# Smaller trips through HBM for the turned hidden rows, queued splits of q and k, and bias tiles loaded on another queue

## The chip, the cores and the metric

The kernel runs on one core of a Trainium2 chip. The metric is the device time of one execution in microseconds, as the median of several. The core has a matrix engine (TensorE, PE in the rows), three engines for the rest (VectorE or DVE, ScalarE or ACT, GpSimd or POOL), an engine that only issues transfers here (SyncE or SP), and 16 DMA engines that all queues share. Each engine works off its own list of instructions in order. A DMA is issued by one of the engines: SP loads the weights, ACT and POOL issue the others.

## The reference

Two networks stand behind each other, of two layers each, on 256 positions of width 1024, all in float32. A layer is a feed-forward part with factor 0.5, a mixer, and a second feed-forward part, each added to the stream x:

```python
def swiglu(x, w_in, w_out):
    gu = x @ w_in                        # 1024 -> 2 x 2816
    g, u = jnp.split(gu, 2, axis=-1)
    return (jax.nn.silu(g) * u) @ w_out  # 2816 -> 1024

x = x + 0.5 * swiglu(rms_norm(x, ffn1_norm[l]), ffn1_w_in[l], ffn1_w_out[l])
x = x + mixer(rms_norm(x, mix_norm[l]), mix_w_in[l], ...)
x = x + 0.5 * swiglu(rms_norm(x, ffn2_norm[l]), ffn2_w_in[l], ffn2_w_out[l])
```

There are thus eight feed-forward parts. The mixer of the first network projects x to q, k, v (512 columns each), to the input of a Fourier part and to two gates, and its attention over 8 heads adds a learned table before the softmax:

```python
s = jnp.einsum('brjqhd,brjuvhd->brjhquv', qg, k_win) * scale + bias[None]  # bias gathered from rpb
s = jnp.where(col_ok, s, -jnp.inf)
p = jax.nn.softmax(s, axis=-1)
```

The mixer of the second network (three kinds of attention) is not touched by the change.

## The kernel before

A product of float32 matrices is made of three matmuls on operands split in a high and a low half (`mm3`, L143). For the weights, `unit` (L111) loads 4 rows of 128 of k by 512 columns into a tile `raw` on SP's queue, and for each pair of k, called a weight tile here, ACT casts the high half `whi` (L341) and DVE subtracts it for the low half `wlo` (L342). `whi` and `wlo` have four buffers each in the parts that matter, so ACT's next cast waits until TensorE is through with an older tile. A weight tile feeds 12 matmuls of 512 columns. SP's loads go ahead as far as the pool of `raw`, four tiles, allows.

**Ticks.** Work that needs no TensorE is queued with `later(fn, ticks)` (L66). Each weight tile is one tick: `advance` (L69) runs at most one entry that is due. `drain` (L62) runs all that is left. What is run at a tick is only recorded there: a scheduler fixes the final order of each engine's list when the program is built.

**The turn.** The second product of a feed-forward part needs h = silu(g)·u with its 2816 columns on the partitions. `turned` (L86) does this without TensorE: DVE transposes blocks of 32×32 into `hB` (L94, one per half t of the positions, one buffer), POOL writes `hB` to HBM (`hop`, L96), and POOL reads it back in the other arrangement (`hT`, L97). That is a trip. `queue_t` (L76) queues the splits `hhi` (ACT, L341) and `hlo` (DVE, L342) of what came back, 7 ticks later. `queue_x` (L201) does the same for half of x between the parts.

**The feed-forward part** (`ffn`, L244). Six chunks of columns of h, five of 512 and one of 256; a chunk of 512 takes 8 weight tiles, four for g and four for u. `GROUPS` (L18) says at which chunk a new tile of h begins: chunks 0 and 1 are turned together, 2 and 3 together (2048 columns of `hB`, 1 MB each way), 4 and 5 alone. `sl` (L272) is silu(g) on ACT, and `h` (L274) its product with u on DVE. The second product has 22 rows of k of h for each half of the output columns; it is written as 16, a drain, and 6.

**The neighbourhood mixer** (`mixer1`). For each pair of heads p, `bias1` (L428) loads a part of the learned table with four DMAs on ACT's queue into a tile `rawb` of the weights' own `raw` pool, and adds the mask on DVE at once (L439). Pairs 0 and 1 are made before the projections, 2 and 3 inside the attention loop. q and k make trips as h does, into `qT` and `kT`; their splits (`qh`, `kzh` on ACT, `kq` on DVE) stand after the drain that ends the projections, though the scheduler may bring them forward.

Of the kernel before, what the change touches and what calls it, by code (L numbers as in the profile page):

```python
# [10 lines left out]
F32 = mybir.dt.float32  # L11
# [3 lines left out]
ALU = mybir.AluOpType  # L15
AX = mybir.AxisListType.X

GROUPS = (0, 2, 4, 5)  # L18
P = 128
T = 2  # L20
D = 1024
# [5 lines left out]
class Net:  # L27
# [46 lines left out]
                return fn()  # L74

    def queue_t(self, h, nk, hhi, hlo, k0):  # L76
        hv = self.turned(lambda t: h[t], nk, self.b("hT", n=2048))
        lag = 7 if nk > 2 else 6
        step = min(nk, 4)
        for i in range(0, nk, step):  # L80
            for t in range(T):
                o = lambda d: d[:, k0 + i : k0 + i + step, t * P : (t + 1) * P].rearrange(
                    "p k (q j) -> p k q j", j=32)
                self.later(lambda hi=o(hhi), lo=o(hlo), s=hv[:, i : i + step, t]: self.split(hi, lo, s), lag)

    def turned(self, src, nk, tile):  # L86
        nc = self.nc
        n = nk * 256
        hop = self.hop.tile([4, P, nk * 64], F32, name=self.nm("hop"), tag=f"hop{nk}")
        hb = self.b("hB", n=2048, bufs=1)[:, :n]  # L90
        ov = hb.rearrange("p (c k t j) -> p k c t j", c=4, t=T, j=32)

        def turn(t):
            nc.vector.transpose(ov[:, :, :, t, :], src(t)[:, : nk * P].rearrange("p (k i c) -> p k c i", c=4, i=32))  # L94
            if t == T - 1:
                nc.gpsimd.dma_start(out=hop.rearrange("q (i c) n -> (q i) (c n)", c=4), in_=hb)  # L96
                nc.gpsimd.dma_start(out=tile[:, :n].rearrange("p (q n) -> p q n", q=4),  # L97
                                    in_=hop.rearrange("q p n -> p q n"))

        for t in range(T):  # L100
            self.later(lambda t=t: turn(t))
        return tile[:, :n].rearrange("p (q k t j) -> p k t q j", q=4, t=T, j=32)
# [98 lines left out]
    def queue_x(self, li):  # L201
        hv = self.turned(lambda t: self.x[:, t, :512], 4, self.xtile())

        def part(k):
            g = self.gcol[:, li, k : k + 1] if isinstance(li, int) else li[:, k : k + 1]
            for t in range(T):
                o = lambda d: d[:, k, t * P : (t + 1) * P].rearrange("p (q j) -> p q j", j=32)
                self.split(o(self.xhi), o(self.xlo), hv[:, k, t], scale=g)

        for k in range(4):  # L210
            self.later(lambda k=k: part(k), 7)

    def xt_half(self, n, li):
        nc = self.nc
# [29 lines left out]
    def ffn(self, w_in, w_out, nxt):  # L244
        nc = self.nc
        rs = None
        self.open()
        self.xtile = lambda: self.b("hT", n=2048)
        self.more(2)
        hhi = self.big.tile([P, 22, T * P], F32R, name=self.nm("hhi"), tag="hhi")  # L250
        hlo = self.big.tile([P, 22, T * P], F32R, name=self.nm("hlo"), tag="hlo")
        self.hold = True
        for c in range(6):
            if c < 5:
                pg = self.dense(self.xhi, self.xlo, KD, [(w_in, c * 512, 512)])
                pu = self.dense(self.xhi, self.xlo, KD, [(w_in, DFF + c * 512, 512)])
                w = 512
                gs, us = pg, pu
            else:
                pp = self.dense(self.xhi, self.xlo, KD, [(w_in, 2560, 256), (w_in, DFF + 2560, 256)])  # L260
                w = 256
                gs, us = pp, [q[:, 256:512] for q in pp]
            if rs is None:
                rs = self.rstd()
            if c == 0:
                self.hold = False
                self.drain()
            if c in GROUPS:
                h, c0 = [self.b("h", n=1024, bufs=4) for _ in range(T)], c
            for t in range(T):  # L270
                sl = self.b("sl", bufs=3)
                nc.scalar.activation(sl[:, :w], gs[t][:, :w], AF.Silu, scale=rs[:, t : t + 1])  # L272
                o = (c - c0) * 512
                nc.vector.scalar_tensor_tensor(h[t][:, o : o + w], us[t][:, :w], rs[:, t : t + 1], sl[:, :w],  # L274
                                               op0=ALU.mult, op1=ALU.mult)
            if c == 5 or c + 1 in GROUPS:
                self.queue_t(h, (o + w) // P, hhi, hlo, c0 * 4)
        for n in range(2):
            ps = self.dense(hhi, hlo, 16, [(w_out, n * 512, 512)], last=False)
            self.drain()  # L280
            self.dense(hhi, hlo, 6, [(w_out, n * 512, 512)], ps=ps, k0=16, first=False)
            for t in range(T):
                xs = self.x[:, t, n * 512 : (n + 1) * 512]
                nc.vector.scalar_tensor_tensor(xs, ps[t], 0.5, xs, op0=ALU.mult, op1=ALU.add)
            self.after(n, nxt)
        self.xtile = None
        self.more(0)
        self.close()
# [120 lines left out]
class Mix1:  # L409
# [18 lines left out]
    def bias1(self, l, p):  # L428
        nc = self.nc
        rp = self.a["rpbp"]  # L430
        bt = self.raw.tile([P, 4, 512], F32, name=self.nm("rawb"), tag="raw").rearrange("p a b -> p (a b)")[:, :768]
        bv = bt.rearrange("p (h e k) -> p h e k", h=2, e=6)
        for half in range(2):
            for h in range(2):
                src = bass.AP(tensor=rp.tensor, offset=((l * 8 + 2 * p + h) * 15 + 5 - half) * 127,
                              ap=[[1, 64], [127, 6], [1, 64]])
                nc.scalar.dma_start(out=bv[half * 64 : half * 64 + 64, h], in_=src)
        bias = self.big.tile([P, 768], F32, name=self.nm("bias"), tag="bias", bufs=3)
        nc.vector.tensor_tensor(bias.rearrange("p (h k) -> p h k", k=64)[:, :, ::-1],  # L439
                                bt.rearrange("p (h k) -> p h k", k=64),  # L440
                                self.cmask.unsqueeze(1).broadcast_to([P, 12, 64]), op=ALU.add)
        return bias

    def mixer1(self, l, nxt):
        nc, a, tc = self.nc, self.a, self.tc
# [12 lines left out]
        qh, vn = tl("qh", [P, 4, 256], F32R), tl("vn", [P, T, 512])  # L458
        u = big.tile([P, KD, 256], F32R, name=self.nm("u"), tag="mhi").rearrange("p (h t a) b -> p h t (a b)", h=2, t=2)
        uhi, ulo = u[:, 0], u[:, 1]  # L460
        bt = [self.bias1(l, p) for p in range(2)]
        self.zpad(kzh.bitcast(F32))
        self.zpad(kzl.bitcast(F32))
        rs = rq = None
        for c in range(4):
            ps = self.dense(self.xhi, self.xlo, KD, [(w_in, c * 512, 512)])
            if c == 0:
# [3 lines left out]
            if c < 2:  # L471
                h = []
# [6 lines left out]
                        nc.vector.tensor_scalar(out=ht, in0=ps[t], scalar1=sc, scalar2=None, op0=ALU.mult)  # L479
                    h.append(ht)  # L480
                turned = self.turned(lambda t, h=h: h[t], 4, qT if c == 0 else kT)
                qv, kv = (turned, None) if c == 0 else (qv, turned)
            elif c == 2:
                for t in range(T):
                    sc = rs[:, t : t + 1]
# [8 lines left out]
                    nc.vector.scalar_tensor_tensor(ulo[:, t], ps[t], sc, uhi[:, t].bitcast(F32),  # L494
                                                   op0=ALU.mult, op1=ALU.subtract)
        self.drain()
        for t in range(T):
            o = lambda d: d[:, :, t * P : (t + 1) * P].rearrange("p k (q j) -> p k q j", j=32)
            self.split(o(qh), o(ql), qv[:, :, t])
            for i in range(2):  # L500
                r = slice(64 * i, 64 * i + 64)
                self.split(o(kzh[:, :, i])[r], o(kzl[:, :, i])[r], kv[r, :, t])
        ohi, olo = tl("ohi", [P, 4, 256], F32R), tl("olo", [P, 4, 256], F32R)
        for p in range(4):
            if p % 2 == 0:
                ona = self.b("ona").rearrange("p (t c) -> p t c", t=T)
            for t in range(T):
                sc = self.psum(self.at)
                e0 = (2 - 2 * t) * 64
                tq = slice(t * P, (t + 1) * P)  # L510
                self.mm3(sc, 512, qh[:, p, tq], ql[:, p, tq], flat(kzh[:, p]), flat(kzl[:, p]), True, True)
                bias = [bt[p][:, h * 384 + e0 : h * 384 + e0 + 256] for h in range(2)]
                po, rc = self.attend(sc, 2, lambda j, st: vn[:, st, (2 * p + j) * 64 : (2 * p + j + 1) * 64], bias)
                nc.vector.tensor_tensor(ona[:, t, (p % 2) * P : (p % 2 + 1) * P].rearrange("p (j d) -> p j d", j=2),
                                        po, rc.unsqueeze(2).broadcast_to([P, 2, 64]), op=ALU.mult)
            if p < 2:
                bt.append(self.bias1(l, p + 2))
            if p % 2 == 1:
                self.tr4(lambda j, t: ona[:, t, j * P : (j + 1) * P],
                         ohi[:, p - 1 : p + 1, :].rearrange("p a b -> p (a b)"),  # L520
                         olo[:, p - 1 : p + 1, :].rearrange("p a b -> p (a b)"))
# [646 lines left out]
```

## Time and profile before

| | before |
| --- | --- |
| median of 3 runs, us | 2278.05 (2275.5, 2278.05, 2285.15) |
| the profiled execution, us | 2291.64 |
| its span, us | 2289.8 |
| granted TensorE clock, mean | 0.996 |
| busy: TensorE / VectorE / ScalarE / GpSimd | 99% / 68% / 50% / 3% |
| chain that ended last: TensorE, issue, DMA | 85%, 7%, 5% |
| of it the trips: hT from hop, hop from hB | 2%, 2% |

The profiled execution lies 13.6 us above the median of the runs. Busy time of TensorE is modelled, since matmuls overlap; how many were started in a stretch tells more than its share. The granted clock is a share of full speed: 1.00 is 2.4 GHz, 0.50 is 1.2 GHz.

### The profile page before, as it was taken

The numbers are of one execution on the slowest core, as the hardware profiler recorded it, in microseconds if no ns is written. First come the engines' busy times: TensorE is split into PE (matmuls) and PEld (weight loads), VectorE is DVE, ScalarE is ACT, GpSimd is POOL, SyncE is SP. The second block draws the span as 40 slices with busy tenths as digits, with TensorE's granted clock in tenths as the row PEclk, the third lists the DMA queues.
The fourth block names the chain that finished last, engine by engine and source line by source line (L and its number), as shares of the span: only waits on it lengthen the run. The fifth ranks groups of instructions, "written<-read, shape, count | busy, mean of one in ns | idle before, by whom it ended". The sixth has DMA issues, their size and how long they took to land.

```text
span 2289.8 us, 27621 instructions
## 1 busy us (share of the span) xinstructions
PE 2260.2 (99%) x10446; PEld 1861.1 (81%) x10446; DVE 1547.2 (68%) x2549; ACT 1148.8 (50%) x1674; POOL 78.3 (3%) x133
## 2 busy tenths in 40 slices
PE   9999999999999999999999999999999999999999
PEld 7877888888788888887888887787887888778787
DVE  5666766666576776666666896765656668877564
ACT  5445545445444555445544555544444455455443
POOL 0001000000000000000000000000000000000000
PEclk9999999999999999999999999999999999999999
DMA  7767555776676745676766533467666755325673
GB/s 263 250 230 231 176 167 181 250 246 204 210 258 208 233 160 180 229 259 209 238 233 214 181 117 129 137 211 241 230 202 224 254 185 174 119 89 198 214 254 130
DMA packets 241669, 464.68 MB, mean 203 GB/s; under 512 B 22176, under 2 KB 47392, under 8 KB 239488
## 3 DMA queue, kind: packets, MB, share of 16 engines
q1 hardware_dynamic: 212272, 397.44, 52.6%
q0 software_dynamic: 14320, 60.69, 7.4%
q10 hardware_dynamic: 14944, 4.79, 1.1%
q8 instruction: 82, 1.34, 0.2%
q14 instruction: 51, 0.42, 0.1%
HBM read 433.00 MB, written 29.88 MB: 202 GB/s over the span
## 4 chain that ended last, share of the span: by engine, by line
PE 85%; issue 7%; DMA 5%; ACT 2%; DVE 1%; ACTq 0%; DVEq 0%; POOLq 0%
PE ps L146 26%; PE ps L145 26%; PE ps L147 26%; DMA hT<-hop 2%; PE ps L403 2%; DMA hop<-hB 2%; PE ps L396 1%; PE ps L891 1%; ACT whi L341 1%; DVE wlo L342 1%; PE ps L683 1%; PE ps L220 1%; PE ps L836 0%; PE ps L240 0%; ACT hhi L341 0%
## 5 line engine op out<-in xcount | busy, mean ns | idle before, releaser
L342 DVE TENSOR_TENSOR wlo<-raw,whi 128x1024 fp32r<-128x1024 f32 (+2 forms) x754 | 906.4, 1210 | 540.0 <-ACT whi L341 522.2
L341 ACT CAST whi<-raw 128x1024 fp32r<-128x1024 f32 (+2 forms) x754 | 777.9, 1044 | 780.9 <-PE ps L147 730.5
L146 PE MATMUL ps<-wlo,xhi 128*128 128x512 f32 (+2 forms) x2048 | 800.3, 392 | 8.3 <-DVE wlo L342 8.2
L145 PE MATMUL ps<-whi,xhi 128*128 128x512 f32 (+2 forms) x2048 | 786.2, 393 | 8.8 <-ACT whi L341 8.4
L147 PE MATMUL ps<-whi,xlo 128*128 128x512 f32 (+2 forms) x2048 | 789.6, 390 | 0.0
L146 PEld LDWEIGHTS ps<-wlo,xhi 128*128 128x128 f32 x2048 | 386.4, 189 | 90.8 <-DVE wlo L342 12.4
L145 PEld LDWEIGHTS ps<-whi,xhi 128*128 128x128 f32 x2048 | 385.3, 189 | 90.2 <-ACT whi L341 11.3
L147 PEld LDWEIGHTS ps<-whi,xlo 128*128 128x128 f32 x2048 | 386.6, 189 | 77.8 <-issue 0.5
L146 PE MATMUL ps<-wlo,hhi 128*128 128x512 f32 x704 | 273.9, 389 | 0.0
L147 PE MATMUL ps<-whi,hlo 128*128 128x512 f32 x704 | 273.9, 389 | 0.0
L145 PE MATMUL ps<-whi,hhi 128*128 128x512 f32 x704 | 271.3, 389 | 0.0
L145 PEld LDWEIGHTS ps<-whi,hhi 128*128 128x128 f32 x704 | 132.1, 188 | 27.6
L146 PEld LDWEIGHTS ps<-wlo,hhi 128*128 128x128 f32 x704 | 132.1, 188 | 27.4
L147 PEld LDWEIGHTS ps<-whi,hlo 128*128 128x128 f32 x704 | 132.1, 188 | 27.3
L94 DVE STREAM_TRANSPOSE hB<-h 128x1024 f32<-128x1024 f32 (+2 forms) x72 | 98.8, 1385 | 5.7 <-DMA hop<-hB 5.4
L342 DVE TENSOR_TENSOR hlo<-hT,hhi 128x512 fp32r<-128x512 f32 (+1 forms) x96 | 58.4, 643 | 56.5 <-ACT hhi L341 56.2
L341 ACT CAST hhi<-hT 128x512 fp32r<-128x512 f32 (+1 forms) x96 | 49.8, 582 | 87.8 <-DMA hT<-hop 87.8
L272 ACT ACTIVATE sl<-ps,rstd 128x512 f32<-128x512 f32 (+1 forms) x96 | 62.3, 651 | 50.9 <-PE ps L147 46.8
L96 POOL DMA_DIRECT2D hop<-hB x43 | 23.6, 548 | 1756.9 <-ACT whi L341 862.3
L391 ACT ACTIVATE pr<-ms,nmx 128x256 f32<-128x256 f32 (+1 forms) x112 | 51.3, 460 | 43.5 <-DVE nmx L386 38.7
L274 DVE SCALAR_TENSOR_TENSOR h<-ps,rstd,sl 128x512 f32<-128x512 f32 (+1 forms) x96 | 65.1, 697 | 2.9 <-PE ps L147 1.8
L97 POOL DMA_DIRECT2D hT<-hop x39 | 29.6, 758 | 184.6 <-DMA hop<-hB 103.6
(352 smaller groups left out, 1707.1 us busy)
## 6 DMA issues: line engine op xcount, KB each, us to landing
raw<-in_ffn_w_gu_dram SPq DMA_DIRECT2D x80, 1024.0 KB, 5.2
raw<-in_ffn_w_in_dram SPq DMA_DIRECT2D x79, 1024.0 KB, 5.2
raw<-in_ffn_w_out_dram SPq DMA_DIRECT2D x40, 1024.0 KB, 5.3
raw<-in_ffn_w_down_dram SPq DMA_DIRECT2D x40, 1024.0 KB, 5.1
raw<-in_mix_w_in_dram SPq DMA_DIRECT2D x32, 1024.0 KB, 6.5
raw<-in_w_gate_dram SPq DMA_DIRECT2D x24, 1024.0 KB, 5.2
hop<-hB POOLq DMA_DIRECT2D x16, 1024.0 KB, 5.9
hT<-hop POOLq DMA_DIRECT2D x16, 1024.0 KB, 6.2
```

What stands on the lines that cost most here:

```text
L94: nc.vector.transpose(ov[:, :, :, t, :], src(t)[:, : nk * P].rearrange("p (k i c) -> p k c i", c=4, i=32))
L96: nc.gpsimd.dma_start(out=hop.rearrange("q (i c) n -> (q i) (c n)", c=4), in_=hb)
L97: nc.gpsimd.dma_start(out=tile[:, :n].rearrange("p (q n) -> p q n", q=4), in_=hop.rearrange("q p n -> p q n"))
L145: mm(ps[:, :n], lhsT=lh, rhs=hi, start=start, stop=False)
L146: mm(ps[:, :n], lhsT=lh, rhs=lo, start=False, stop=False)
L147: mm(ps[:, :n], lhsT=ll, rhs=hi, start=False, stop=stop)
L272: nc.scalar.activation(sl[:, :w], gs[t][:, :w], AF.Silu, scale=rs[:, t : t + 1])
L274: nc.vector.scalar_tensor_tensor(h[t][:, o : o + w], us[t][:, :w], rs[:, t : t + 1], sl[:, :w], op0=ALU.mult, op1=ALU.mult)
L341: self.nc.scalar.copy(hi, src)
L342: return self.nc.vector.tensor_sub(lo, src, hi.bitcast(F32))
L391: nc.scalar.activation(pr[:, s], src[:, s], AF.Exp, bias=nm[:, j : j + 1], accum_out=den[:, j : j + 1])
L403: nc.tensor.matmul(po[:, j * 64 : (j + 1) * 64], lhsT=pt[:, q], rhs=v(j, st), start=(st == 0), stop=(st == ns - 1))
```

## The change

Every chunk of h is turned by its own trip: `GROUPS` holds all six, a trip of chunks 0 to 3 is 512 KB each way instead of 1 MB for two chunks, and `hT`, `hB` and `h` are half as wide. The lag of the splits is 8 ticks everywhere. The second product is one run of 22 rows without the drain in it. In the mixer, `rawb` becomes a tile of its own with one buffer, its DMAs go to POOL's queue, the mask addition is a step of its own (`mask1`) that is queued at ticks 6 and 10, then stands after the drain and after the first pair of heads, and each starts the next pair's load. The splits of q are queued at 9 ticks and those of k at 7.

```diff
-GROUPS = (0, 2, 4, 5)
+GROUPS = (0, 1, 2, 3, 4, 5)
...
-        hv = self.turned(lambda t: h[t], nk, self.b("hT", n=2048))
-        lag = 7 if nk > 2 else 6
+        hv = self.turned(lambda t: h[t], nk, self.b("hT", n=1024))
+        lag = 8
...
-        hb = self.b("hB", n=2048, bufs=1)[:, :n]
+        hb = self.b("hB", n=1024, bufs=1)[:, :n]
...
-            self.later(lambda k=k: part(k), 7)
+            self.later(lambda k=k: part(k), 8)
...
-                h, c0 = [self.b("h", n=1024, bufs=4) for _ in range(T)], c
+                h, c0 = [self.b("h", bufs=4) for _ in range(T)], c
...
-            ps = self.dense(hhi, hlo, 16, [(w_out, n * 512, 512)], last=False)
-            self.drain()
-            self.dense(hhi, hlo, 6, [(w_out, n * 512, 512)], ps=ps, k0=16, first=False)
+            ps = self.dense(hhi, hlo, 22, [(w_out, n * 512, 512)])
...
-        bt = self.raw.tile([P, 4, 512], F32, name=self.nm("rawb"), tag="raw").rearrange("p a b -> p (a b)")[:, :768]
+        bt = self.b("rawb", 768, 1)
...
-                nc.scalar.dma_start(out=bv[half * 64 : half * 64 + 64, h], in_=src)
+                nc.gpsimd.dma_start(out=bv[half * 64 : half * 64 + 64, h], in_=src)
+        return bt
+
+    def mask1(self, bt):
...
-        bt = [self.bias1(l, p) for p in range(2)]
+        bt, rb = [], [self.bias1(l, 0)]
+
+        def masked():
+            bt.append(self.mask1(rb.pop()))
+            if len(bt) < 4:
+                rb.append(self.bias1(l, len(bt)))
+
+        for n in (6, 10):
+            self.later(masked, n)
...
+                    for t in range(T):
+                        self.later(lambda t=t: split_q(t), 9)
...
+                    for t in range(T):
+                        self.later(lambda t=t: split_k(t), 7)
...
         self.drain()
-        for t in range(T):
-            o = lambda d: d[:, :, t * P : (t + 1) * P].rearrange("p k (q j) -> p k q j", j=32)
-            self.split(o(qh), o(ql), qv[:, :, t])
...
+        masked()
...
-            if p < 2:
-                bt.append(self.bias1(l, p + 2))
+            if p == 0:
+                masked()
```

ScalarE's list in the first feed-forward part, where the second trip of before is split (chunks 2 and 3, `hT_798`) and where the one of chunk 3 is after (`hT_818`). Before:

```order
L341 CAST whi_883<-raw_877 128x1024
L341 CAST whi_913<-raw_911 128x1024
L272 ACTIVATE sl_951<-ps_801,rstd_306 128x512
L341 CAST whi_919<-raw_911 128x1024
L272 ACTIVATE sl_954<-ps_802,rstd_306 128x512
L341 CAST whi_965<-raw_962 128x1024
L341 CAST hhi_150<-hT_798 128x4x128 x4
L341 CAST whi_971<-raw_962 128x1024
L341 CAST whi_1004<-raw_1001 128x1024
```

After:

```order
L339 CAST whi_905<-raw_899 128x1024
L339 CAST whi_935<-raw_933 128x1024
L272 ACTIVATE sl_971<-ps_821,rstd_306 128x512
L339 CAST whi_939<-raw_933 128x1024
L272 ACTIVATE sl_974<-ps_822,rstd_306 128x512
L339 CAST hhi_150<-hT_818 128x4x128 x2
L339 CAST whi_985<-raw_982 128x1024
L339 CAST whi_991<-raw_982 128x1024
L339 CAST whi_1023<-raw_1020 128x1024
```

Four casts that stood behind the first weight tile after the two `sl` are now two, directly behind the second `sl`.

GpSimd's list in the first neighbourhood mixer, from the clearing of `kzh` and `kq` (MEMSET) to the trip of k. Before:

```order
L349 MEMSET kzh_1499 64x4x256
L350 MEMSET kzh_1499 64x4x256
L349 MEMSET kq_1500 64x4x256
L350 MEMSET kq_1500 64x4x256
L96 DMA hop_1619<-hB_1620 128x1024
L97 DMA qT_1501<-hop_1619 128x4x256
L546 DMA h_2276<-in_mix_gate_bias_dram 128x512
L546 DMA h_2352<-in_mix_gate_bias_dram 128x512
L546 DMA h_2428<-in_mix_gate_bias_dram 128x512
L96 DMA hop_1699<-hB_1700 128x1024
L546 DMA h_2504<-in_mix_gate_bias_dram 128x512
L97 DMA kT_1502<-hop_1699 128x4x256
```

After, from the last MEMSET on (four loads of `rawb_1524`, the first pair's, stand ahead of the MEMSETs):

```order
L348 MEMSET kq_1518 64x4x256
L435 DMA rawb_1645<-in_rpbp_dram 64x6x64 x4
L96 DMA hop_1628<-hB_1629 128x1024
L435 DMA rawb_1732<-in_rpbp_dram 64x6x64 x4
L566 DMA h_2294<-in_mix_gate_bias_dram 128x512
L566 DMA h_2370<-in_mix_gate_bias_dram 128x512
L97 DMA qT_1519<-hop_1628 128x4x256
L566 DMA h_2446<-in_mix_gate_bias_dram 128x512
L96 DMA hop_1715<-hB_1716 128x1024
L566 DMA h_2522<-in_mix_gate_bias_dram 128x512
L435 DMA rawb_1888<-in_rpbp_dram 64x6x64 x4
L97 DMA kT_1520<-hop_1715 128x4x256
```

Three groups of four loads now stand between the trips of q and k, and the trip back of k is the last of them all.

VectorE's list in the same mixer, from the third chunk's tiles on: `bias` is the mask addition, `kq` the low halves of q and k. Before:

```order
L479 TENSOR_SCALAR h_1697<-ps_1622,rstd_1597 128x512
L94 STREAM_TRANSPOSE hB_1700<-h_1695 128x4x4x32
L94 STREAM_TRANSPOSE hB_1700<-h_1697 128x4x4x32
L342 TENSOR_TENSOR wlo_1748<-raw_1741,whi_1747 128x1024
L342 TENSOR_TENSOR kq_1500<-qT_1501,qh_1503 128x4x128 x2
L439 TENSOR_TENSOR bias_1923<-rawb_1918,cmask 128x12x64
L342 TENSOR_TENSOR wlo_1782<-raw_1779,whi_1781 128x1024
L342 TENSOR_TENSOR wlo_1786<-raw_1779,whi_1785 128x1024
L342 TENSOR_TENSOR wlo_1816<-raw_1813,whi_1815 128x1024
L489 TENSOR_SCALAR vn_1504<-ps_1702,rstd_1597 128x512
L342 TENSOR_TENSOR wlo_1820<-raw_1813,whi_1819 128x1024
```

After:

```order
L497 TENSOR_SCALAR h_1713<-ps_1631,rstd_1606 128x512
L94 STREAM_TRANSPOSE hB_1716<-h_1711 128x4x4x32
L340 TENSOR_TENSOR wlo_1771<-raw_1761,whi_1770 128x1024
L94 STREAM_TRANSPOSE hB_1716<-h_1713 128x4x4x32
L340 TENSOR_TENSOR wlo_1805<-raw_1802,whi_1804 128x1024
L340 TENSOR_TENSOR wlo_1811<-raw_1802,whi_1810 128x1024
L441 TENSOR_TENSOR bias_1886<-rawb_1732,cmask 128x12x64
L340 TENSOR_TENSOR wlo_1843<-raw_1840,whi_1842 128x1024
L514 TENSOR_SCALAR vn_1522<-ps_1718,rstd_1606 128x512
L340 TENSOR_TENSOR wlo_1851<-raw_1840,whi_1850 128x1024
L340 TENSOR_TENSOR kq_1518<-qT_1519,qh_1521 128x4x128 x2
```

The third pair's mask addition stands two weight tiles later than before, and the split of q, which stood ahead of it, four tiles later.

## Rows read from the trace of the kernel before

**Rows 1.** Stretches of 15 us: busy time and instruction count of each engine, TensorE's granted clock.

```profile
80.00:95.00 15.00, 15.00 (x68) 12.43 (x67) 7.75 (x8) 7.19 (x8) 0.00 (x0) 1.00 0.79 271
116.00:131.00 15.00, 12.89 (x56) 10.14 (x55) 11.12 (x13) 7.13 (x9) 0.45 (x1) 1.00 0.49 165
225.00:240.00 15.00, 12.24 (x47) 9.60 (x46) 8.69 (x10) 7.12 (x11) 0.76 (x1) 0.89 0.98 282
603.00:618.00 15.00, 12.60 (x42) 9.53 (x42) 9.76 (x11) 7.64 (x10) 0.00 (x0) 0.77 0.42 140
728.00:743.00 15.00, 13.88 (x60) 10.90 (x59) 12.02 (x27) 7.21 (x12) 0.14 (x1) 1.00 0.88 328
1556.00:1571.00 15.00, 13.30 (x57) 10.44 (x56) 10.98 (x12) 9.79 (x12) 0.00 (x0) 1.00 0.58 193
1738.00:1753.00 15.00, 12.79 (x49) 9.91 (x48) 9.76 (x11) 7.96 (x10) 0.00 (x0) 0.89 0.47 146
2166.00:2181.00 15.00, 12.16 (x53) 9.48 (x52) 10.79 (x12) 8.27 (x11) 0.00 (x0) 1.00 0.48 156
```

**Rows 2.** Waits of TensorE: us in total, times, longest.

```profile
PE ps L145 <- ACT whi L341: 8.9, 9, 2.1
PE ps L146 <- DVE wlo L342: 8.2, 9, 2.8
```

**Rows 3.** Waits of ScalarE, the same columns.

```profile
ACT hhi L341 <- DMA hT<-hop: 87.8, 32, 6.0
```

**Rows 4.** ScalarE's timeline, first FFN: start, us, instruction, count, idle before and releaser.

```profile
110.26 0.68 ACT L272 ACTIVATE sl<-ps,rstd 128x512 f32<-128x512 f32 x1
114.75 1.05 ACT L341 CAST whi<-raw 128x1024 fp32r<-128x1024 f32 x1 [3.80 <-PE ps L147]
119.68 2.18 ACT L341 CAST hhi<-hT 128x512 fp32r<-128x512 f32 x4 [3.87 <-DMA hT<-hop]
121.77 1.99 ACT L341 CAST whi<-raw 128x1024 fp32r<-128x1024 f32 x2
```

**Rows 5.** TensorE's timeline, same stretch.

```profile
118.63 0.39 PE L145 MATMUL ps<-whi,xhi 128*128 128x512 f32 x1
...
122.86 0.49 PE L145 MATMUL ps<-whi,xhi 128*128 128x512 f32 x1 [1.35 <-ACT whi L341]
```

**Rows 6.** VectorE's timeline, first FFN: end of the fourth chunk, a subtraction, turn of the fifth.

```profile
97.94 1.41 DVE L274 SCALAR_TENSOR_TENSOR h<-ps,rstd,sl 128x512 f32<-128x512 f32 x2
...
125.25 1.22 DVE L342 TENSOR_TENSOR wlo<-raw,whi 128x1024 fp32r<-128x1024 f32 x1
...
128.17 2.08 DVE L94 STREAM_TRANSPOSE hB<-h 128x512 f32<-128x512 f32 x2
```

**Rows 7.** ScalarE's timeline, the fifth chunk's split.

```profile
139.71 1.15 ACT L341 CAST hhi<-hT 128x512 fp32r<-128x512 f32 x2 [4.55 <-DMA hT<-hop]
```

**Rows 8.** The same turn and split in a later FFN, on VectorE and ScalarE.

```profile
1180.95 2.08 DVE L94 STREAM_TRANSPOSE hB<-h 128x512 f32<-128x512 f32 x2
...
1194.20 1.14 ACT L341 CAST hhi<-hT 128x512 fp32r<-128x512 f32 x2 [6.05 <-DMA hT<-hop]
```

**Rows 9.** VectorE's groups by form: busy us, mean ns.

```profile
L94 DVE STREAM_TRANSPOSE hB<-h 128x512 f32<-128x512 f32 x24 | 25.0, 1077 | 0.0
```

**Rows 10.** Second neighbourhood mixer: VectorE's turn of k.

```profile
748.64 2.07 DVE L94 STREAM_TRANSPOSE hB<-h 128x512 f32<-128x512 f32 x2
```

**Rows 11.** The DMA issued at 757.11 us in that mixer.

```profile
kT<-hop POOLq DMA_DIRECT2D x1, 512.0 KB, 8.5
```

**Rows 12.** First neighbourhood mixer, VectorE's timeline: a mask addition.

```profile
227.97 0.96 DVE L439 TENSOR_TENSOR bias<-rawb,cmask 128x768 f32<-128x768 f32 x1 [4.68 <-DMA rawb<-in_rpbp_dram]
```

**Rows 13.** Tile rawb: DMA to landing.

```profile
DMA to landing us min/median/max: 2.7/4.2/11.4
```

**Rows 14.** TensorE's timeline in the first attention.

```profile
270.99 0.44 PE L396 MATMUL ps<-ident,pr 128*128 128x128 f32 x2 [0.86 <-ACT pr L391]
```

**Rows 15.** Tile hT: durations in ns (min/median/max) of its DMA issues on GpSimd.

```profile
L97 POOL DMA_DIRECT2D hT<-hop x39: 754/758/766, 67.0 to 2235.1; - x39
```

More of the change, by code (lines that the diff above doesn't have):

```diff
@@ L247, in ffn @@
         self.open()
-        self.xtile = lambda: self.b("hT", n=2048)
+        self.xtile = lambda: self.b("hT", n=1024)
         self.more(2)
@@ L436, in bias1 @@
                               ap=[[1, 64], [127, 6], [1, 64]])
-                nc.scalar.dma_start(out=bv[half * 64 : half * 64 + 64, h], in_=src)
+                nc.gpsimd.dma_start(out=bv[half * 64 : half * 64 + 64, h], in_=src)
+        return bt
+    def mask1(self, bt):
+        nc = self.nc
         bias = self.big.tile([P, 768], F32, name=self.nm("bias"), tag="bias", bufs=3)
@@ L464, in mixer1, with split_k @@
         rs = rq = None
+        part = lambda d, t: d[:, :, t * P : (t + 1) * P].rearrange("p k (q j) -> p k q j", j=32)
+        split_q = lambda t: self.split(part(qh, t), part(ql, t), qv[:, :, t])
+        def split_k(t):
+            for i in range(2):
+                r = slice(64 * i, 64 * i + 64)
+                self.split(part(kzh[:, :, i], t)[r], part(kzl[:, :, i], t)[r], kv[r, :, t])
         for c in range(4):
@@ L481, in mixer1 @@
                 turned = self.turned(lambda t, h=h: h[t], 4, qT if c == 0 else kT)
-                qv, kv = (turned, None) if c == 0 else (qv, turned)
+                if c == 0:
+                    qv = turned
+                    for t in range(T):
+                        self.later(lambda t=t: split_q(t), 9)
+                else:
+                    kv = turned
+                    for t in range(T):
+                        self.later(lambda t=t: split_k(t), 7)
             elif c == 2:
@@ L496, in mixer1 @@
         self.drain()
-        for t in range(T):
-            o = lambda d: d[:, :, t * P : (t + 1) * P].rearrange("p k (q j) -> p k q j", j=32)
-            self.split(o(qh), o(ql), qv[:, :, t])
-            for i in range(2):
-                r = slice(64 * i, 64 * i + 64)
-                self.split(o(kzh[:, :, i])[r], o(kzl[:, :, i])[r], kv[r, :, t])
+        masked()
         ohi, olo = tl("ohi", [P, 4, 256], F32R), tl("olo", [P, 4, 256], F32R)
```

## The prediction, made blind

> **What bounds the kernel now.** I read first how many matmuls TensorE starts in stretches of equal length, because its busy share of 99% is modelled and hides small gaps. An undisturbed stretch of 15 us shows 68 matmuls, and the stretches with a gap 42 to 60 [rows 1]. A matmul is shown 0.39 us long, so a stretch counts those of 15.4 us, and one is started every 15.4 / 68 = 0.2267 us; a weight tile, 12 matmuls, takes 2.72 us. TensorE is the bound nearly everywhere, and what can be won lies in the gaps. Its own waits come next: 8.9 us for `whi` and 8.2 us for `wlo`, nine times each [rows 2]. So it never waits for a trip directly, but for a cast or subtraction that stands behind something else on ScalarE or VectorE. ScalarE's waits then name what: 87.8 us for `hT`, in 32 places [rows 3]. Only a few of these 32 cost TensorE anything, and the timeline of one shows when.
>
> In the first FFN ScalarE casts a weight tile at 114.75, then stands at the four `hhi` casts until the trip lands, 3.87 us, casts them in 2.18 us, and casts the next tile only at 121.77 [rows 4]. The tile that begins at 118.63 is used up 2.72 us later, at 121.4 and TensorE starts again at 122.86, 1.35 us of waiting by its own row, with a second wait for `wlo` behind [rows 5]. The cast of 114.75 feeds a tile that begins at 118.63: it was ready 3.88 − 1.05 = 2.8 us early. That is the reserve; a wait within it costs nothing, and a longer one stops TensorE.
>
> **The change part by part.**
>
> *Trips of the wide groups.* Five stretches hold such a gap (116, 603, 1556, 1738 and 2166 us). Missing matmuls against 68: 12 + 26 + 11 + 19 + 15 = 83, or 83 × 0.2267 = 18.8 us; The 26 at 603 are 5.9 us, more than any single wait of TensorE [rows 2]; there the granted clock of the stretch is 0.77, and at 1738 it is 0.89 [rows 1]. The clock fell to its half level for some microseconds behind the gap, and those are in the sum.
>
> Would the gaps go? After the change a chunk's splits are two casts (1.15 us [rows 7]) and stand directly behind the second `sl`, ahead of the next weight tile, not behind it. In the frame of rows 4 this `sl` ends at 110.94, and ScalarE then idled 3.80 us up to the cast of 114.75, because TensorE had not released the buffer [rows 4]. So a landing up to 114.75 − 1.15 = 113.6 costs nothing at all, and up to 2.8 us later, 116.4, nothing on TensorE. When does it land? The chunk's product `h` begins at 97.94 [rows 6]; two of these (1.41), two transposes of 1.08 [rows 9] and, by the new order, one weight tile's subtraction (1.22 [rows 6]) between them put the end of the turn at about 102.7. The fifth chunk already travels alone: turned by 130.25, split from 139.71 [rows 6, 7], a trip of 9.4 us. It is the shortest of the six of its kind that can be followed; the longest is turned at 1180.95 + 2.08 = 1183.03 and split at 1194.20, 11.2 us [rows 8]. Landing is then 112.1 to 113.9, ahead of or just past the free limit and 2.5 us ahead of the costly one. The limit on a trip is 116.4 − 102.7 = 13.7 us. ScalarE will still wait in these places, up to about 3 us, in a gap that it has anyway.
>
> So I take all five gaps off: −18.8 us. Bounds: 0 (other waits come up in their place) to −18.8.
>
> The rest of this part is off the path. VectorE runs twice as many transposes of half the width (1.08 us each [rows 9]) on the same bytes, hidden by its waits for ScalarE. GpSimd issues 32 more writes and 32 more reads; it has little else to do. The lag of 8 and the second product without a drain leave the splits of chunks 4 and 5 and of x where they stood, by the new order.
>
> *The mixer's bias.* In the first mixer VectorE stands 4.68 us at a mask addition whose load has not landed, with the next weight tile's subtraction behind it [rows 12]; TensorE waits for that, its longest wait, 2.8 us [rows 2], and the clock falls to half behind it (0.89 over the stretch). That stretch misses 21 matmuls, and the one at 728, where ScalarE waits for a late weight load because bias tiles hold the weights' buffers, 8 [rows 1]: 29 × 0.2267 = 6.6 us. After the change the bias has its own tile, so weights load as far ahead as elsewhere. The third pair's load starts when the second mask is done, four weight tiles (10.9 us) ahead of its own mask, with one trip out ahead of it on GpSimd. The landing of such a load was 4.2 us at the median and 11.4 at worst [rows 13]. At the median it is in time by some 5 us. I take −6.6; bounds 0 and −6.6, and above zero by the third rival.
>
> *Queued splits of q and k.* The split of k moves from behind the 85th weight tile to behind the 88th. TensorE's first score product follows it, so about 33 matmuls (7.5 us) which stood between the softmax steps now run ahead of them. Attention already waits for a softmax once, 0.86 us [rows 14]. With less between the steps it will wait more: between 0 and 7.5 us for each of two mixers. I take 1.5, nearest to the row of 0.86 and above it: +3.0 for both.
>
> *New small waits.* Trips are twice as many and start at more moments, beside weight loads. I add +2 (bounds 0 and +8: a fifth of the 40 trips of 512 KB at 0.9 to 1.0 us, the mean of TensorE's waits [rows 2]).
>
> On these trips the Trainium skill has a rule that speaks against the change. The 39 trips' read issues on GpSimd took 754 to 766 ns [rows 15], while VectorE was busy two thirds of the time, so none was stretched. The skill's "SBUF — State Buffer", section "🔬 SBUF: two separate sides", says that a DMA issued from GpSimd can wait for its descriptors while VectorE runs an operation that holds the port the two share; it gives about 620 ns alone and 3100 ns beside such a copy. By the page's figures each trip of two issues would be some 5 us longer, an estimate; by the row nothing is added. I go by the row.
>
> **Sum.** −18.8 − 6.6 + 3.0 + 2.0 = −20.4 us against the profiled execution of 2291.64: 2271.2. The runs' median is 13.6 us lower. If every run has the same gaps, the median becomes 2278.05 − 20.4 = 2257.7. If all of the 13.6 us is gaps that this one execution had beyond an ordinary run, only 25.4 − 13.6 = 11.8 remain to be won, less 5 of cost: 2271.2. Five of the wide trips are late and the rest are not, so how many are late will differ from run to run; I take the middle, 2264.5.
>
> **The rivals.**
>
> *A trade.* The five gaps go, but attention without its filling takes near its bound (5 us a mixer), or the clock falls to half there, and the small waits reach 8: −25.4 + 10 + 8 = −7.4, from 2278.05 at most 2270.7, and with half of the excess of the profile 2277. For it speaks that the filler is certainly moved; against it, that the only wait seen there is 0.86 us. About 2273.
>
> *Crowded trips.* The trip of k in the second mixer ended its turn at 750.71, was issued back at 757.11 and landed 8.5 us later, at 765.6 [rows 10, 11]: 14.9 us for 512 KB, beside bias and weight loads. That is over the limit of 13.7. If the 32 trips of chunks 0 to 3 were so, each would stop TensorE (14.9 − 13.7) + 0.9 for the late `wlo` (8.2 / 9 [rows 2]), 2.1 us, +67 in all: 2264.5 + 67 = 2331. It decides from a trip of 13.7 us on, and some ten such trips would eat the gain. Against it: none of the FFN's single trips was above 11.2.
>
> *The bias behind the queue (slower).* GpSimd's list in the mixer now holds three groups of four bias loads between the turns, and the trip back of k stands behind the last, which waits for the third mask. If bias loads take the worst 11.4 us [rows 13], with the issue and the write ahead of them, the third mask is about 4 us late, and VectorE and k's trip behind it as much. One such stop cost 21 missing matmuls, 4.8 us, in the first mixer [rows 1]; two in each mixer, for the mask and for k, are +19, and the −6.6 is partly lost: 2264.5 + 19 + 4 = 2287. It decides when such a load takes over about 9 us. For it: beside q's trip and weight loads one load took that long; against it: the median load of 4.2 us.
>
> *Stretched issues.* If VectorE did hold up GpSimd's issues, by a run of three subtractions (3.5 us) each, a trip would be 7 us longer, 15 to 18: 32 × about 3.7 = +118, 2382. Against it stand the 39 issues of unchanged length [rows 15]. The rule of the Trainium skill's page named above would act in this way.
>
> **How the numbers follow.** What a measurement of this kernel can tell from no change is about 0.5%, 11.4 us: faster is under 2266.7, slower over 2289.4. Forecast 0.55, a trade 0.29, the bias behind the queue 0.08, crowded trips 0.05, stretched issues 0.03. Of the forecast's own range, 2255 to 2272, three parts in four are faster (0.42), and a tenth of the trade too, with some of the cases where more late trips are ordinary than I see (0.08 in sum): faster 0.50. Slower: both trip cases and a third of the bias case, 0.10. The same: 0.40. The time of the likeliest is 2264. The range reaches to the forecast's lower end with the runs at their slower, and up over the trade: 2251 to 2280.
>
> **What would show it.** In the profile after: matmul counts of 66 to 68 in each 15 us of the FFNs' first products; ScalarE's waits for `hT` still there, more in number and shorter, none above 5 us ahead of a weight tile that TensorE waits for; TensorE's waits for `whi` under 3 us in sum; no mask addition of VectorE waiting for `rawb`; TensorE waiting for `pr` some 3 us more than before. I am wrong if TensorE stops behind `hhi` again, if a trip of a chunk takes over 13.7 us, if the wait for `kT` or for a mask appears ahead of a weight tile, or if the gaps go and the median does not move: then an ordinary run did not have them.

## The result: slower, and the profile after

| | before | after |
| --- | --- | --- |
| median, us | 2282.34 (6 runs, 2275.5 to 2285.15) | 2307.26 (6 runs, 2300.19 to 2312.11) |
| ratio after / before | | 1.0109, 95% interval 1.0089 to 1.0128 |
| the profiled execution: time, span, us | 2291.64, 2289.8 | 2301.41, 2299.6 |

The change costs 25 us; I had forecast a gain of 14 (from 2278.05, the median of the first three runs of before, to 2264) and a range that ended at 2280.

The same table as [rows 1], of stretches of the profile after (TensorE's matmul count is the first number in brackets, the granted clock the first number behind the last bracket):

```profile
616.00:631.00 15.00, 13.50 (x58) 10.28 (x57) 11.18 (x12) 7.62 (x9) 0.56 (x1) 1.00 0.46 138
641.00:656.00 15.00, 13.41 (x51) 10.29 (x50) 10.72 (x12) 7.04 (x8) 0.56 (x1) 0.89 0.41 132
1172.00:1187.00 15.00, 12.85 (x55) 9.75 (x54) 11.95 (x13) 8.10 (x9) 0.54 (x1) 1.00 0.41 140
2193.00:2208.00 15.00, 12.34 (x52) 9.35 (x51) 11.56 (x12) 8.10 (x9) 0.54 (x1) 1.00 0.38 113
220.00:235.00 15.00, 15.00 (x67) 12.42 (x67) 10.16 (x11) 7.74 (x10) 4.50 (x7) 1.00 1.03 306
```

The last stretch holds the first mixer's mask addition: 67 matmuls where 47 stood, no gap. The four above are in feed-forward parts, with 51 to 58 matmuls: gaps like those of [rows 1] are still there, and there are more of them, ten behind `hhi` casts for five. TensorE's waits, which answer to [rows 2] (us in total, times, longest):

```profile
PE ps L145 <- ACT whi L339: 11.6, 13, 1.8
PE ps L146 <- DVE wlo L340: 9.1, 13, 0.8
...
PE ps L145 <- ACT oTc L241: 2.1, 1, 2.1
PE ps L394 <- ACT pr L389: 1.7, 2, 0.9
```

And the wait of ScalarE that answers to [rows 3]:

```profile
ACT hhi L339 <- DMA hT<-hop: 235.4, 48, 8.9
```

ScalarE now waits for `hT` in 48 places, not 32, and 235.4 us, not 87.8; the mean wait has grown from 2.7 to 4.9 us. TensorE's waits for `whi` and `wlo` together are 20.7 us in place of 17.1. The wait for `pr` (1.7) is what it was before.

How these waits come about shows in one feed-forward part, the first of the second network. ScalarE's timeline, the casts of chunks 0 to 3, each behind the first `sl` of the chunk that follows (start, us, instruction, idle before and releaser):

```profile
1095.37 0.69 ACT L272 ACTIVATE sl<-ps,rstd 128x512 f32<-128x512 f32 x1 [0.99 <-PE ps L147]
...
1101.34 1.14 ACT L339 CAST hhi<-hT 128x512 fp32r<-128x512 f32 x2 [3.65 <-DMA hT<-hop]
...
1117.13 0.69 ACT L272 ACTIVATE sl<-ps,rstd 128x512 f32<-128x512 f32 x1 [0.98 <-PE ps L147]
...
1124.36 1.14 ACT L339 CAST hhi<-hT 128x512 fp32r<-128x512 f32 x2 [4.92 <-DMA hT<-hop]
...
1138.89 0.69 ACT L272 ACTIVATE sl<-ps,rstd 128x512 f32<-128x512 f32 x1 [0.98 <-PE ps L147]
...
1148.71 1.14 ACT L339 CAST hhi<-hT 128x512 fp32r<-128x512 f32 x2 [7.50 <-DMA hT<-hop]
...
1162.79 0.69 ACT L272 ACTIVATE sl<-ps,rstd 128x512 f32<-128x512 f32 x1 [0.98 <-PE ps L147]
...
1173.48 1.14 ACT L339 CAST hhi<-hT 128x512 fp32r<-128x512 f32 x2 [8.38 <-DMA hT<-hop]
```

VectorE's second transposes of the same four chunks, the end of each turn:

```profile
1088.33 1.11 DVE L94 STREAM_TRANSPOSE hB<-h 128x512 f32<-128x512 f32 x1
...
1110.90 1.07 DVE L94 STREAM_TRANSPOSE hB<-h 128x512 f32<-128x512 f32 x1
...
1133.93 1.11 DVE L94 STREAM_TRANSPOSE hB<-h 128x512 f32<-128x512 f32 x1
...
1158.26 1.10 DVE L94 STREAM_TRANSPOSE hB<-h 128x512 f32<-128x512 f32 x1
```

TensorE in the stretch where it stops:

```profile
1150.85 0.50 PE L145 MATMUL ps<-whi,xhi 128*128 128x512 f32 x1 [0.44 <-ACT whi L339]
1152.11 0.50 PE L146 MATMUL ps<-wlo,xhi 128*128 128x512 f32 x1 [0.76 <-DVE wlo L340]
...
1175.62 0.49 PE L145 MATMUL ps<-whi,xhi 128*128 128x512 f32 x1 [1.31 <-ACT whi L339]
1176.88 0.50 PE L146 MATMUL ps<-wlo,xhi 128*128 128x512 f32 x1 [0.77 <-DVE wlo L340]
```

From the end of the turn to the cast the four trips take 1101.34 − 1089.44 = 11.9, 12.4, 13.7 and 14.1 us. At the same time the turns end later: the `sl` that TensorE releases half a chunk on comes 5.9 us behind the end of the first turn, 5.2 behind the second, 3.9 and 3.4 behind the third and fourth. Both drift the same way, and the wait grows from 3.65 to 8.38 us. The waits of 3.65 and 4.92 cost TensorE nothing; behind those of 7.50 and 8.38 it waits 0.44 + 0.76 and 1.31 + 0.77 us. The cost is more than these waits: from first `sl` to first `sl` a chunk takes 21.76 us where nothing stops (1095.37, 1117.13, 1138.89), and 23.90 over the first stop, 2.1 us more for 1.2 us of waiting. Over the ten stops of this profile that distance grows by 1.8 to 4.3 us, 29 us in sum; over the five of the profile before it is 18.6. In all eight parts the first trip is 11.2 to 11.9 us, and the longest 12.3 to 15.0.

What moved beside the first trip, from the DMA issues between 1089 and 1096 us (count, KB each, median us from issue to landing):

```profile
raw<-in_ffn_w_gu_dram SPq DMA_DIRECT2D x1, 1024.0 KB, 6.9
hop<-hB POOLq DMA_DIRECT2D x1, 512.0 KB, 5.4
hT<-hop POOLq DMA_DIRECT2D x1, 512.0 KB, 5.9
```

And beside the fourth, between 1159 and 1166 us:

```profile
raw<-in_ffn_w_down_dram SPq DMA_DIRECT2D x2, 1024.0 KB, 8.4
raw<-in_ffn_w_gu_dram SPq DMA_DIRECT2D x1, 512.0 KB, 7.0
hop<-hB POOLq DMA_DIRECT2D x1, 512.0 KB, 5.6
hT<-hop POOLq DMA_DIRECT2D x1, 512.0 KB, 7.6
```

The way back took 7.6 us there for 5.9. Over their whole length both trips have two weight loads that start beside them; what differs is when. The loads that start beside the fourth trip are in SyncE's timeline:

```profile
1161.73 4.45 SPq L118 DMA_DIRECT2D raw<-in_ffn_w_down_dram  x2
```

The first of the two starts 2.4 us behind the turn's end (1159.36). Beside the first trip it is 3.5 us (1092.95 against 1089.44).

### The profile page after: what moved, and what is told of

The parts are those of the page before. It is cut to its first block, busy times and chain, and to the rows that moved or that the text cites. A ratio compares the mean times of both kernels' runs of the same rounds, so it can differ in the third digit from the quotient of the medians.

```text
span 2299.6 us, 27743 instructions
## 1 busy us (share of the span) xinstructions
PE 2263.2 (98%) x10446; PEld 1857.2 (81%) x10446; DVE 1545.5 (67%) x2581; ACT 1145.6 (50%) x1674; POOL 120.3 (5%) x197
## 5 line engine op out<-in xcount | busy, mean ns | idle before, releaser
L339 ACT CAST hhi<-hT 128x512 fp32r<-128x512 f32 (+1 forms) x96 | 51.4, 582 | 235.4 <-DMA hT<-hop 235.4
L96 POOL DMA_DIRECT2D hop<-hB x59 | 32.4, 549 | 1627.7 <-DVE hB L94 988.8
L94 DVE STREAM_TRANSPOSE hB<-h 128x512 f32<-128x512 f32 (+1 forms) x104 | 105.4, 1014 | 16.1 <-DMA hop<-hB 15.6
L97 POOL DMA_DIRECT2D hT<-hop x55 | 41.5, 755 | 283.3 <-DMA hop<-hB 128.2
```

The source lines that it names most:

```text
L339: self.nc.scalar.copy(hi, src)
```

## The experiments

All ratios are to the kernel before on the same chip (ffn_only, held10 and halfw ran on one chip, the other four on another). "Held" below means: ScalarE's casts of a trip get an edge in the order behind a later weight cast, so that they can't be moved up.

**The feed-forward part alone** (`ffn_only`: the functions from `bias1` to the end of `mixer1` as before the change).

> The mixer and its bias are those of before, the feed-forward part is that of after. Theory 1 (the loss lies in the feed-forward parts, whose 512 KB trips land 11 to 14 us after the turn, at or over the limit): slower than before by the whole loss and what the mixer gave, +25 to +33 us, 2307 to 2315. Rival (the queue of GpSimd in the mixer costs the loss): within 8 us of before, 2274 to 2290.

Measured: 2307.02 us (4 runs, 2303.21 to 2308.77), ratio 1.0117 (1.0096 to 1.0137). The whole loss lies in the feed-forward parts. What the mixer part was to give did not appear: with the old mixer the time is the same as with the new one. The first mixer has no gap here even with its old bias: the stretch that held 47 matmuls before holds 68, and TensorE has no wait for `whi` or `wlo` between 103 and 465 us.

```profile
225.00:240.00 15.00, 15.00 (x68) 12.41 (x67) 9.62 (x11) 8.17 (x10) 0.76 (x1) 1.00 1.09 332
```

**The casts held two weight tiles later** (`held10`).

```diff
+            self.cast = nc.scalar.copy(hi[:, :m, :off], raw[:, j : j + m, :off])
...
-        lag = 8
+        lag = 10 if k0 < 16 else 8
+
+        def behind(hi, lo, s):
+            with self.tc.issue_after(self.cast.ins):
+                self.split(hi, lo, s)
```

In the last line of `queue_t`, `behind` takes the place of `self.split` for `k0 < 16`, which is chunks 0 to 3. The lag and the edge came together here; no run shows what either does alone.

> As after, but the casts of chunks 0 to 3 are held on ScalarE behind a weight tile two places later, 5.4 us later. Theory 1: a trip of up to 14 us has then landed, ScalarE's waits for hT in these places go, and with them the stops of TensorE in the feed-forward parts; 2307 - 25 to - 40, so 2267 to 2282. Rival (the number of trips and transposes itself costs, through the DMA engines or VectorE): no change from after, 2300 to 2312.

Measured: 2268.07 us (6 runs, 2267.33 to 2270.32), ratio 0.9950 (0.9937 to 0.9963), 39 us below the feed-forward part of the change as it was (ffn_only on the same chip). It keeps the other edits of that part (the narrower trips, the second product in one run), so these alone cause no loss. ScalarE's timeline in the same feed-forward part, a first `sl` and a first cast, twice, the casts with no wait ahead of them:

```profile
1105.86 0.69 ACT L278 ACTIVATE sl<-ps,rstd 128x512 f32<-128x512 f32 x1 [0.76 <-PE ps L153]
...
1114.30 0.61 ACT L345 CAST hhi<-hT 128x512 fp32r<-128x512 f32 x1
...
1149.38 0.69 ACT L278 ACTIVATE sl<-ps,rstd 128x512 f32<-128x512 f32 x1 [0.76 <-PE ps L153]
...
1157.82 0.61 ACT L345 CAST hhi<-hT 128x512 fp32r<-128x512 f32 x1
```

VectorE's turns of chunks 1 and 3 in it:

```profile
1098.61 2.05 DVE L99 STREAM_TRANSPOSE hB<-h 128x512 f32<-128x512 f32 x2
...
1142.12 2.05 DVE L99 STREAM_TRANSPOSE hB<-h 128x512 f32<-128x512 f32 x2
```

ScalarE's waits for `hT` in the whole run, all of them at chunks 4 and 5:

```profile
ACT hhi L345 <- DMA hT<-hop: 47.1, 16, 5.1
```

TensorE's waits, as in [rows 2]:

```profile
PE ps L151 <- ACT whi L138: 1.1, 3, 0.6
...
PE ps L152 <- DVE wlo L139: 0.4, 1, 0.4
```

TensorE's two waits are 1.5 us together. The turn of chunk 1 ends at 1100.66, 5.2 us ahead of the `sl` at 1105.86, that of chunk 3 at 1144.17, 5.2 ahead of 1149.38: nothing drifts. Trips of chunks 0 to 3 took 11.0 to 12.5 us in all parts, shorter than the 11.2 to 15.0 of after though only the casts were moved. So the length of a trip is not its own. That it depends on ScalarE's wait for the one before became theory 2. The weight loads beside the trip of chunk 3, as above for after:

```profile
1148.55 4.22 SPq L123 DMA_DIRECT2D raw<-in_ffn_w_down_dram  x2
```

The first starts 4.4 us behind the turn's end (1144.17), for 2.4 in after. Against the `sl` it starts at nearly the same time, 0.83 us ahead (1.06 in after): the turn moved, and not the load.

**Half of the weight loads left out** (`halfw`). In the feed-forward parts every second load of four rows of k is left out and the tile loaded before is used again.

```diff
-        raw = self.raw.tile([P, 4, 512], F32, name=self.nm("raw"), tag="raw")
+        again = getattr(self, "kept", None) if self.xtile and nk == 4 and len(segs) == 1 else None
+        raw = again or self.raw.tile([P, 4, 512], F32, name=self.nm("raw"), tag="raw")
...
-                nc.sync.dma_start(
+                again or nc.sync.dma_start(
...
+        self.kept = raw if self.xtile and nk == 4 and len(segs) == 1 and step == 4 and not again else None
```

> As after, but in the feed-forward parts every second weight tile of four rows is not loaded and the one before it is used again: half of the weight traffic is left out, the work of all engines is the same. Theory 1 in the form that trips are long because they share the DMA engines with weight loads: a trip then takes 8 to 9.5 us and the stops go, 2262 to 2278. Rival (a trip's time is its own: issue, two latencies, small packets): trips stay at 11 to 14 us, time 2300 to 2312.

Measured: 2273.95 us (11 runs, 2272.33 to 2275.22), ratio 0.9973 (0.9964 to 0.9982). The stops behind `hhi` are gone. The trips of chunks 0 to 3 are 10.0 to 11.2 us, and 7.9 to 12.6 in the first part, not the 8 to 9.5 I expected; it is the way back that shrank. DMA issues of this kernel (KB each, median us to landing):

```profile
hop<-hB POOLq DMA_DIRECT2D x51, 512.0 KB, 4.9
...
hT<-hop POOLq DMA_DIRECT2D x47, 512.0 KB, 4.3
```

The same of the changed kernel:

```profile
hop<-hB POOLq DMA_DIRECT2D x51, 512.0 KB, 5.6
...
hT<-hop POOLq DMA_DIRECT2D x47, 512.0 KB, 5.8
```

The way back fell from 5.8 to 4.3 us, the way out from 5.6 to 4.9. ScalarE's waits for `hT` fell too, to 78.6 us, so against after two things changed. Against held10, which has all loads and no such wait, only the way back is shorter (4.3 for 6.1; the way out 4.9 for 4.3). Part of a trip is what it shares with the weights, and a part is its own. The run lies 6 us above held10; its profile has two waits of 2.1 us for `oTc` in the second network's mixers where held10 has one, and behind each of the two the granted clock falls to 1.2 GHz for 3.4 us. The stretch behind the first of them, in halfw and then in held10, where the clock stays up:

```profile
1438.00:1446.00 8.00, 7.21 (x24) 5.77 (x25) 5.07 (x8) 3.17 (x5) 0.00 (x0) 0.79 0.40 131
1437.00:1445.00 8.00, 7.24 (x31) 5.93 (x32) 6.64 (x10) 4.74 (x7) 0.00 (x0) 1.00 0.37 132
```

Seven matmuls fewer are about 1.6 us; the second wait has a drop of the same length behind it.

**Every second wait held** (`held_even`).

```diff
-        lag = 10 if k0 < 16 else 8
+        held = k0 in (0, 8)
+        lag = 10 if held else 8
```

> As held10, but only chunks 0 and 2 have their casts held 5.4 us later; chunks 1 and 3 are cast where the changed kernel casts them. Theory 2 (a wait of ScalarE for one trip delays its weight casts, the weight loads then come bunched and collide with the next trip, so the trips grow from chunk to chunk): with the wait before it gone, the trips of chunks 1 and 3 take 11 to 12 us as in held10, their waits are 3 to 4 us and cost TensorE next to nothing; 2266 to 2276. Rival (a trip is long or short by its place alone, chunk 3 by the loads of the second product's weights): chunk 3's trips stay at 13 to 15 us, and half or more of the loss stays, 2282 to 2300.

Measured: 2269.08 us (6 runs, 2267.32 to 2275.48), ratio 0.9948 (0.9933 to 0.9964). Chunks 1 and 3 are cast where the changed kernel casts them, and with no wait in the chunk ahead of theirs they wait 3.4 to 4.2 us, near the 3.0 to 3.7 of a first chunk after the change, where chunk 1 waited 3.2 to 5.4 us and chunk 3 5.6 to 8.5. Chunk 3 of the fourth feed-forward part waited 8.47 us after the change. ScalarE's timeline shows it here:

```profile
972.53 1.14 ACT L346 CAST hhi<-hT 128x512 fp32r<-128x512 f32 x2 [3.38 <-DMA hT<-hop]
```

VectorE's turn of that chunk:

```profile
959.58 2.05 DVE L100 STREAM_TRANSPOSE hB<-h 128x512 f32<-128x512 f32 x2
```

Its trip takes 972.53 − 961.63 = 10.9 us. The rival, that a chunk's place sets its trip, falls. The same run shows the other side: the trips of chunk 2, which stand behind the waits of chunk 1, took 12.2 to 13.8 us, for 11.0 to 11.4 in held10, though their own casts are held.

**ScalarE delayed, without any trip** (`busy_act`): held10, and one copy of 128×6656 on ScalarE behind the `sl` of chunks 1 to 4.

```diff
+            if 0 < c < 5:
+                junk = self.b("junk", n=13 * 512, bufs=1, dt=mybir.dt.bfloat16)
+                nc.scalar.copy(junk.rearrange("p (a b) -> p a b", a=13), sl.unsqueeze(1).broadcast_to([P, 13, 512]))
```

> As held10, with one copy of 128x6656 on ScalarE, about 5.7 us by the rate of its 512-wide casts, at the place where the changed kernel casts the trips of chunks 0 to 3; it waits for no trip. Theory 2: a delay of ScalarE's weight casts alone, without any wait for a trip, makes the trips of the next chunks grow to 13 us or more. TensorE stays within its reserve of 2.8 us, so the time moves little, 2268 to 2285. Rival (it is the trip itself that sets its length): trips stay at 11.0 to 11.9 us as in held10, time 2266 to 2275.

Measured: 2267.39 us (4 runs, 2266.14 to 2267.77), ratio 0.9936 (0.9920 to 0.9951). The copy takes 5.74 us. ScalarE's timeline in the fourth feed-forward part:

```profile
943.99 0.69 ACT L278 ACTIVATE sl<-ps,rstd 128x512 f32<-128x512 f32 x1 [1.21 <-PE ps L153]
...
946.34 5.74 ACT L284 CAST junk<-sl 128x6656 bf16<-128x6656 f32 x1
...
955.24 0.62 ACT L348 CAST hhi<-hT 128x512 fp32r<-128x512 f32 x1 [1.25 <-DMA hT<-hop]
```

VectorE's turn of chunk 2 there:

```profile
939.36 1.11 DVE L99 STREAM_TRANSPOSE hB<-h 128x512 f32<-128x512 f32 x1
```

The turn of chunk 2 ends at 940.47, now 3.5 us ahead of the `sl` behind it (5.2 in held10), and the trip lands at 955.24, 14.8 us on, late even for the held cast. The trips of chunks 2 and 3 are 12.9 to 14.9 us in every feed-forward part, while those of the first chunk, with no copy ahead of them, stay at 11.7 to 12.1. Chunk 1, behind a single copy, is mixed: 13.8 to 14.7 us in three parts and 11.2 to 12.2 in five. A third weight load starts 6.5 us behind the start of its write in all eight parts; where the way back was issued behind that load (at 6.7 to 7.4 us) it took 6.7 to 7.2 us, and where ahead of it (5.6 to 5.9) 5.0 to 6.1. These five also have the copy running beside their trip, as the long ones have, so it is not the copy as such that slows a transfer. A delay of ScalarE by itself thus lengthens the trips that follow, always from the second copy on; no wait for a trip is needed for it. The time, just under what theory 2 gave and within the rival's range, does not suffer: TensorE's waits for `whi` and `wlo` are 1.9 us in sum. I put that down to the held casts, which no longer stand ahead of a weight tile that TensorE is about to need.

**The wide groups with held casts** (`wide_held`): the kernel before, with the edge and the lag of 10 for its two groups.

```diff
-        lag = 7 if nk > 2 else 6
+        lag = 10 if k0 < 16 else 7 if nk > 2 else 6
```

`behind` and its use are those of held10.

> The kernel before, with its wide groups, but the casts of the two groups of chunks held behind a weight tile one to four places later, one at a time. Theory 1 (what counts is only whether the cast stands behind the landing): the five late groups no longer stop TensorE, a gain of 10 to 19 us, 2262 to 2271, as far as the first mixer's gap stays. Rival (smaller trips are needed as well): within 5 us of before, 2276 to 2286.

Measured: 2266.97 us (5 runs, 2265.93 to 2267.35), ratio 0.9934 (0.9920 to 0.9948). Smaller trips are not needed for the gain. The four longest trips of the wide groups are 15.0 to 15.7 us here too, in the places where they are long before, though no wait of ScalarE for an earlier trip of their part precedes them. So theory 2 does not account for these, which are among the five that opened the gaps of before; what makes them long was not tried.

**The old mixer with held casts** (`held_oldmix`).

> As held10, with the mixer and its bias as before the change. My term for the mixer was -6.6 us and +3 for attention: then 2268 + 3.6 = 2272, and the mask addition or a late weight load stops TensorE in one of the two mixers. Rival (the mixer's gap came from the late loads behind a disturbed feed-forward part): no gap in either mixer, 2266 to 2270.

Measured: 2267.43 us (6 runs, 2266.69 to 2267.73), ratio 0.9936 (0.9922 to 0.9950), 0.6 us below held10, on another chip. The mixer's part of the change gives nothing that can be measured. Half of each guess holds: the first mixer's gap is not there, the second has one at 718 us, two waits of 0.25 and 0.76 us and 61 matmuls in the stretch, about 1.6 us.

```profile
715.00:730.00 15.00, 13.99 (x61) 10.98 (x60) 12.12 (x27) 7.30 (x12) 0.23 (x1) 1.00 0.88 327
```

The new mixer lacks it, but all runs with it have a wait of 2.1 us for `oTc` in the second network's mixer which those with the old one haven't.

held10, busy_act, wide_held and held_oldmix all beat both kernels by the same 0.5 to 0.7% of the one before and can't be told apart; the simplest is wide_held, the kernel before with the edge alone.

## Why the prediction was wrong, step by step

**The limit was right.** I put the last harmless landing at 116.4, 7.8 us behind the first `sl` of that chunk (108.63), or a trip of 13.7 us. In the rows above the casts that begin 6.0 and 7.2 us behind their `sl` cost TensorE nothing, and those at 9.8 and 10.7 us do. Over all 32 places of the profile after, none up to 8.1 us stopped TensorE and all from 9.4 us did, ten of them; in trips, none up to 13.1 us and all from 13.5.

**The length of the trip was the step that failed.** I took 9.4 to 11.2 us from chunk 4 [rows 6 to 8]. The first trips of chunks 0 to 3 took 11.2 to 11.9 us, and later ones to 15.0. The trips I chose were the same size, but at another place, beside the loads of the second product's weights. At the place of chunks 0 to 3 they are 11.0 to 12.5 us even in held10, where ScalarE waits for none of them.

**And a wait called free was not.** I wrote that ScalarE "will still wait in these places, up to about 3 us, in a gap that it has anyway". With trips of 11.9 us the first cast comes at 1101.34, and with its 1.14 us it runs past the gap by about a microsecond (the gap of 3.80 us against a wait of 3.65 and the cast). TensorE does not notice. But the weight casts behind it start late and come one upon another, VectorE's subtractions come later and one of them stands between the two transposes of the next turn, which ends later. The weight loads behind the turn nearly keep their time against the `sl` and so start earlier in the trip. In held10 the first load behind the turn starts 4.4 us behind its end in all 24 trips of chunks 1 to 3, in busy_act 2.3 us, in after 2.4 to 4.7; all ten trips that stopped TensorE are among the twelve of after where it was 3.6 us or less. held_even takes the wait away in front of a chunk and the trip is short; busy_act puts the delay in without a wait and the next ones are long. That a delay of ScalarE lengthens the trips and moves the turns behind it is shown by both; the path between them (subtractions, turn, loads) is my reading of the order and of these times. The start of one load does not settle the length alone: with 3.8 to 4.4 us, chunk 2 of held_even took 12.2 to 13.8 us. How much of the growth is due to the loads is open, though halving the loads removed 1.5 us of the way back. With a trip at each chunk the delay has 21.8 us to die out, with the wide groups 43.5; in the profile before, the second wide trips behind waits of 3.5 to 4.6 us took 12.2 to 13.5 us, no longer than the others (12.4 to 15.4). That would let the change be worse than the fewer and longer trips that it replaced; no run varied this distance alone.

**The terms.** Wide groups −18.8: measured as a loss of 26 us (ffn_only against before: 2307.02 to 2281.13). The mixer −6.6: 0 within the noise. The gap of 4.8 us in the first mixer was the profiled execution's own, or hung on what ran before it, since in the profiles of ffn_only, held_oldmix and wide_held, all with the old mixer, TensorE idles 0, 0 and 0.75 us there; the second mixer's gap was real, 1.6 us, and the new wait for `oTc` takes as much. Attention without its filling +3.0: nothing, 1.7 us of waiting for `pr` before and after. New small waits +2: one of 2.1 us for `oTc`. GpSimd issues 16 more writes and 16 more reads (59 for 43, 55 for 39), not the 32 of each that I wrote; no time in the sum rests on it. Stretched issues on GpSimd: no, the way back's issue took 747 to 770 ns in all 55 cases. The rule of the Trainium skill that a DMA issued from GpSimd can wait while VectorE holds the port the two share ("SBUF — State Buffer", section "🔬 SBUF: two separate sides") again does not show here.

**The rivals.** Crowded trips was the one that came, and I gave it 0.05. I named its limit and its price per stop (2.1 us; the ten stops lost 1.8 to 4.3 each), and set it aside because no single trip of the FFN had been above 11.2, the same wrong sample. It came in part: TensorE stopped at ten of the 32 trips. Its time of 2331 was for all.

**The scale.** I set the ordinary run's gaps below the profiled one's by half of 13.6 us. held10 and its kin have hardly any gap and lie at 2267 to 2268, so an ordinary run of before holds about 14 us of removable gaps and not 25.4, near the lower case of 11.8; an ordinary run of after holds about 39. In the profiles, after is 33.8 us longer than held10, and the ten stops make 29 of them.

## What to carry to other kernels

A wait that an engine spends in a gap of its own is free only while what stands behind it starts on time: ask what the delayed engine releases, and what those releases collide with a chunk later. Take a transfer's time from the same place in the loop, with the same loads beside it, not from one of the same size elsewhere. And where a scheduler orders the work, an edge to a later instruction of the same engine holds a cast behind the landing; with it, and the longer lag, the kernel before gained 16 us, which neither half of the change did.

## What the runs showed that I had not expected

A trip of half the bytes is hardly shorter beside the same weight loads: the eleven wide trips of before that were not late took 12.2 to 13.5 us, the trips of half the size 11.0 to 12.5 in held10. Landings of 512 KB had a median of 4.0 and 4.5 us before, and 5.6 and 5.8 after, for the same bytes, once most of them stood in the first product; in held10, at the same places, it was 4.3 out and 6.1 back. The bias loads on GpSimd's queue took 7.0 us at the median, on ScalarE's queue before 4.2 [rows 13], at other places in the mixer.
